# One column of a mean-square kernel loaded ahead of the rest through GpSimd's queue

## The chip, the cores and the metric

The kernel runs on one core of a Trainium2 chip. The core has a matrix engine (unused here), VectorE, ScalarE, GpSimd, SyncE (which only issues transfers here), and 16 DMA engines that move data between the memory (HBM) and the on-chip buffer of 128 partitions. The metric is the device time of one execution in microseconds, as the median of several runs. [...]

## The reference

The input x is 32 x 512 x 1024 values in fp32. For each of the 16,384 rows of 1024 values the variance is wanted:

```
mean_sq = np.mean(x**2, axis=-1)
sq_mean = np.mean(x, axis=-1)**2
return (mean_sq - sq_mean).astype(np.float32)
```

So 67.1 MB are read and 64 KB are written.

## The kernel before, in words

The 16,384 rows are laid out as 128 columns of 128 rows: each partition holds one row (4 KB) of each column. Two blocks give the layout. In the first, 16 columns wide, partition p holds 16 rows of x that follow one another; in the second, 112 columns wide, 112 of them. So `load` (line 40), which loads n neighbouring columns, reads one run of n x 4 KB per partition, 128 runs in all. Every load is issued by SyncE (SP in the profile), in program order, and runs on its queue.

The columns come in two parts. The body is 13 groups of 8 columns (columns 0 to 103), one 4 MB load each, into a pool of three buffers (`xt`). So the load of group g waits until the engines are done with group g - 3. The end is columns 104 to 127, in a buffer of their own (`xt_end`), which no earlier reader holds: loads of 6, 6, 4, 3, 2 and 1 columns (`END_LOADS`, line 62), then columns 126 and 127 as two half loads each.

A column is worked on by VectorE or by ScalarE. VectorE makes statistics of each half of a row (`bn_stats`, line 111), two instructions of 512 elements per column. ScalarE makes two passes over a column (lines 121 and 129): first the negative mean, then the squared deviation, summed into the result tile `mv`. In the body ScalarE takes 3 columns of one group and 2 of the next; in the end the string `END_WHO` says who takes which column (A is ScalarE, D is VectorE); the first of them, column 104, is ScalarE's.

The halves' statistics of the body, and of the first two end loads, are joined into variances by GpSimd in three chains of ten small instructions (`join`, lines 90 to 102): one for the even groups, one for the odd groups, one for the end. For the other end columns VectorE joins them itself (`bn_aggr`, lines 169 and 179).

Two stores write the result: the first block's 16 columns through ScalarE's queue (line 181), the second block's 112 columns through SP's (line 182). In ScalarE's stream the first store stands behind its last body column and ahead of its first end column; it waits for GpSimd's second join, and so does all that follows it on ScalarE. GpSimd issues no transfer; its own stream is four memsets at the start, then the three joins. A scheduler orders each engine's instructions and sets the waits, and it gives the transfers of the SP and ScalarE queues eight completion semaphores in turn, so that a later transfer may wait for the one that used its semaphore before.

Of the kernel before, what the change touches and what calls it, by code (L numbers as in the profile page):

```python
# [11 lines left out]
def kernel(  # L12
# [8 lines left out]
    nc = tc.nc  # L21
    P = nc.NUM_PARTITIONS
# [4 lines left out]
    xf = x.flatten_outer_dims()  # L27
    N, D = xf.shape
# [6 lines left out]
    BLOCKS = [(0, SMALL, 0), (SMALL, ncols - SMALL, SMALL * P)]  # L35

    def block_of(c):
        return next(b for b in BLOCKS if b[0] <= c < b[0] + b[1])

    def load(dst, c0, n, f0=0, f=D):  # L40

        b0, pitch, row0 = block_of(c0)
        assert c0 + n <= b0 + pitch
        ap = [[pitch * D, P], [D, n], [1, f]] if n > 1 else [[pitch * D, P], [1, f]]
        nc.sync.dma_start(  # L45
            out=dst,
            in_=dataclasses.replace(xf, offset=(row0 + c0 - b0) * D + f0, ap=ap),
        )

    def store(engine, block):  # L50
        b0, pitch, row0 = block
        engine.dma_start(
            out=dataclasses.replace(out, offset=row0, ap=[[pitch, P], [1, pitch]]),
            in_=mv[:, 1, b0 : b0 + pitch],
        )
# [3 lines left out]
    END0 = GROUP * NGROUPS  # L59
# [2 lines left out]
    END_LOADS = [6, 6, 4, 3, 2, 1]  # L62
    END_WHO = "AADDDDAADDDDDADDDADADA"
    BATCH = (2, 6, 2)

    xpool = ctx.enter_context(tc.tile_pool(name="xpool", bufs=3))
    spool = ctx.enter_context(tc.tile_pool(name="spool", bufs=4))
# [3 lines left out]
    neg_mean = opool.tile([P, ncols], FP32)  # L71
    junk = [opool.tile([P, D], mybir.dt.bfloat16, name=f"junk{i}") for i in range(4)]
    xt_end = opool.tile([P, ncols - END0, D], FP32)
    stats_of = {}

    def stats_block(name, groups, each):

# [3 lines left out]
    def join(st, groups, each, first, step, skip):  # L81

        n = groups * each
        part = st.rearrange("p n h (e s) -> p n (h e) s", s=3)
        mean, m2 = part[:, :, :, 1], part[:, :, :, 2]
        two = opool.tile([P, n, 2], FP32, name=f"two{first}")
        mu = opool.tile([P, n, 1], FP32, name=f"mu{first}")
        dev = opool.tile([P, n, 4], FP32, name=f"dev{first}")
        g = nc.gpsimd
        g.tensor_tensor(out=two, in0=mean[:, :, 0:2], in1=mean[:, :, 2:4], op=ALU.add)  # L90
        g.tensor_tensor(out=mu, in0=two[:, :, 0:1], in1=two[:, :, 1:2], op=ALU.add)
        g.tensor_scalar(out=mu, in0=mu, scalar1=0.25, scalar2=None, op0=ALU.mult)  # L92
        g.tensor_tensor(out=dev, in0=mean, in1=mu.to_broadcast([P, n, 4]), op=ALU.subtract)  # L93
        g.tensor_tensor(out=dev, in0=dev, in1=dev, op=ALU.mult)  # L94
        g.tensor_scalar(out=dev, in0=dev, scalar1=D / 4.0, scalar2=None, op0=ALU.mult)  # L95
        g.tensor_tensor(out=dev, in0=dev, in1=m2, op=ALU.add)  # L96
        g.tensor_tensor(out=two, in0=dev[:, :, 0:2], in1=dev[:, :, 2:4], op=ALU.add)  # L97
        g.tensor_tensor(out=mu, in0=two[:, :, 0:1], in1=two[:, :, 1:2], op=ALU.add)
        var = mv[:, 1, first : first + groups * step].rearrange(
            "p (g k) -> p g k", k=step  # L100
        )[:, :, skip : skip + each]
        g.tensor_scalar(  # L102
            out=var,
            in0=mu.rearrange("p (g k) o -> p g (k o)", k=each),
            scalar1=1.0 / D,
            scalar2=None,
            op0=ALU.mult,
        )
# [4 lines left out]
    def dve_halves(stats, xcol):  # L113
        dve_half(stats, 0, xcol[:, :H])
        dve_half(stats, 1, xcol[:, H:])

    def act_cols(cols):

        s = D ** -0.5
        for i, (xcol, c) in enumerate(cols):  # L120
            nc.scalar.activation(  # L121
                out=junk[i],
                in_=xcol,
                func=ACTF.Copy,
                scale=-s / D,
                accum_out=neg_mean[:, c : c + 1],
            )
        for i, (xcol, c) in enumerate(cols):
            nc.scalar.activation(  # L129
                out=junk[3],  # L130
                in_=xcol,
                func=ACTF.Square,
                scale=s,
                bias=neg_mean[:, c : c + 1],
                accum_out=mv[:, 1, c : c + 1],
            )
# [6 lines left out]
    for g in range(NGROUPS):  # L143
        c0 = g * GROUP
        xt = xpool.tile([P, GROUP, D], FP32, name="xt")
        load(xt, c0, GROUP)
        skip = ACT_OF_GROUP[g % 2]
        act_cols([(xt[:, k, :], c0 + k) for k in range(skip)])
        st, _, each = body[g % 2]
        for k in range(skip, GROUP):  # L150
            dve_halves(st[:, g // 2 * each + k - skip, :, :], xt[:, k, :])
    for par, (st, groups, each) in enumerate(body):
        join(st, groups, each, par * GROUP, 2 * GROUP, ACT_OF_GROUP[par])

    nb, step, skip = BATCH
    each = step - skip
    st_end = stats_block("stats_end", nb, each)
    k = 0
    for b, n in enumerate(END_LOADS):
        load(xt_end[:, k : k + n, :] if n > 1 else xt_end[:, k, :], END0 + k, n)  # L160
        mine = range(k, k + n)
        act_cols([(xt_end[:, j, :], END0 + j) for j in mine if END_WHO[j] == "A"])
        for j in mine:
            if END_WHO[j] == "D" and b < nb:
                dve_halves(st_end[:, b * each + j - k - skip, :, :], xt_end[:, j, :])
            elif END_WHO[j] == "D":
                stats = spool.tile([P, 2, 6], FP32, name="stats")
                dve_halves(stats, xt_end[:, j, :])
                nc.vector.bn_aggr(out=mv[:, :, END0 + j], in_=stats)  # L169
        if b == nb - 1:  # L170
            join(st_end, nb, each, END0, step, skip)
        k += n
    for j in range(k, ncols - END0):
        stats = spool.tile([P, 2, 6], FP32, name="stats")
        for h in range(2):
            xh = xt_end[:, j, h * H : (h + 1) * H]
            load(xh, END0 + j, 1, h * H, H)
            dve_half(stats, h, xh)
        nc.vector.bn_aggr(out=mv[:, :, END0 + j], in_=stats)  # L179

    store(nc.scalar, BLOCKS[0])
    store(nc.sync, BLOCKS[1])


# [28 lines left out]
```

## Time and profile before

| | us |
|---|---|
| median of 3 runs | 165.49 (165.44 to 165.92) |
| span of the profiled execution | 163.5 |
| VectorE busy | 106.1 (65%) |
| ScalarE busy | 94.9 (58%) |
| GpSimd busy | 10.2 (6%) |
| first body load landed | 12.7 |
| first half of column 126 landed | 157.81 |
| last VectorE instruction ends | 160.84 |
| second store issued | 160.98 |
| second store landed | 162.54 |

The span runs from the first to the last instruction of one execution that the profiler recorded; the runs' median is 2.0 us above it. The busy shares are averages over the whole span. The DMA part of the profile gives the traffic in slices of time, by queue: queue 1 is SP's, queue 10 ScalarE's, queue 14 brings instructions. The packet records give the duration of each row moved, and each of the 16 engines reports the end of its share of a transfer in an event of its own; a transfer has landed with the last of the sixteen. The chain of waits is followed back from the last instruction, at each step to what released it.

### The profile page before, as it was taken

To read this page: it belongs to the slowest core of one execution; us is meant where nothing else is said; L and a number is where in the kernel's file an instruction comes from. 1 tells how busy PE (TensorE), PEld (TensorE's weight loads), DVE (VectorE), ACT (ScalarE), POOL (GpSimd) and SP (SyncE) were. 2 spreads that over 40 slices of the span, in tenths; PEclk is the share of its full clock that TensorE was granted. 3 is DMA by queue.
4 is the path that set the end of the run, shared out by engine and by line. 5 is a ranking of instruction groups with operands and counts; after the bars stand their busy time and mean duration, and the time that the engine had idled before them with its cause. 6 is when DMAs were issued, how large, how long until landed. Compare 5 with 4: busy or idle time off the path is not lost.

```text
span 163.5 us, 462 instructions
## 1 busy us (share of the span) xinstructions
DVE 106.1 (65%) x182; ACT 94.9 (58%) x165; POOL 10.2 (6%) x34
## 2 busy tenths in 40 slices
DVE  0008559393793917949097682949559396859993
ACT  3008756195733937349390693809755195499892
POOL 0000000000000000000000000000000635302200
DMA  7899898998999999999999999999999999999970
GB/s 257 385 481 417 385 513 385 417 481 385 481 417 385 485 409 393 497 393 425 465 393 473 417 393 505 393 401 489 393 465 425 421 391 475 391 440 409 408 291 14
DMA packets 3602, 67.19 MB, mean 411 GB/s; under 512 B 656, under 2 KB 656, under 8 KB 1296
## 3 DMA queue, kind: packets, MB, share of 16 engines
q1 hardware_dynamic: 3456, 67.17, 96.3%
q10 hardware_dynamic: 144, 0.01, 0.1%
q14 instruction: 2, 0.02, 0.0%
HBM read 67.11 MB, written 0.07 MB: 411 GB/s over the span
## 4 chain that ended last, share of the span: by engine, by line
DMA 79%; DVE 11%; ACT 8%; issue 0%; SPq 0%
DMA xt<-in_x_dram 62%; DMA xt_end<-in_x_dram 17%; DVE stats L111 10%; ACT junk L129 4%; ACT junk L121 4%; DVE mv L179 0%; SPq L45 0%
## 5 line engine op out<-in xcount | busy, mean ns | idle before, releaser
L111 DVE BATCH_NORM_STATS2 stats<-xt 128x6 f32<-128x512 f32 x142 | 85.5, 678 | 50.7 <-DMA xt<-in_x_dram 50.7
L121 ACT ACTIVATE junk<-xt 128x1024 bf16<-128x1024 f32 x33 | 34.5, 1046 | 59.2 <-DMA xt<-in_x_dram 59.2
L129 ACT ACTIVATE junk<-xt,neg_mean 128x1024 bf16<-128x1024 f32 x33 | 37.7, 1142 | 0.6
L111 DVE BATCH_NORM_STATS2 stats_end<-xt_end 128x6 f32<-128x512 f32 x16 | 9.7, 680 | 3.7 <-DMA xt_end<-in_x_dram 3.7
L121 ACT ACTIVATE junk<-xt_end 128x1024 bf16<-128x1024 f32 x8 | 8.4, 1046 | 5.0 <-POOL mv L102 4.2
L111 DVE BATCH_NORM_STATS2 stats<-xt_end 128x6 f32<-128x512 f32 x16 | 10.1, 666 | 0.1
L129 ACT ACTIVATE junk<-xt_end,neg_mean 128x1024 bf16<-128x1024 f32 x8 | 9.2, 1144 | 0.2
L90 POOL TENSOR_TENSOR two<-stats 128x72 f32<-128x72 f32 (+1 forms) x2 | 0.8, 406 | 131.3 <-DVE stats L111 131.3
L129 ACT ACTIVATION_READ_ACCUMULATOR junk<-xt,neg_mean 128x1 f32 x33 | 6.2, 186 | 0.0
L121 ACT ACTIVATION_READ_ACCUMULATOR junk<-xt 128x1 f32 x33 | 6.2, 186 | 0.0
L121 ACT ACT_TABLE_LOAD x1 | 1.3, 1283 | 0.7 <-PEq L197 0.7
L121 ACT ACTIVATION_READ_ACCUMULATOR junk<-xt_end 128x1 f32 x8 | 1.5, 186 | 0.0
L129 ACT ACTIVATION_READ_ACCUMULATOR junk<-xt_end,neg_mean 128x1 f32 x8 | 1.5, 186 | 0.0
L95 POOL TENSOR_SCALAR dev<-dev 128x144 f32<-128x144 f32 (+2 forms) x3 | 1.4, 472 | 0.3
L169 DVE BATCH_NORM_AGGREGATE mv<-stats 128x2 f32<-128x12 f32 x6 | 1.2, 203 | 0.1
L94 POOL TENSOR_TENSOR dev<-dev 128x144 f32<-128x144 f32 (+2 forms) x3 | 1.1, 362 | 0.2
L96 POOL TENSOR_TENSOR dev<-dev,stats 128x144 f32<-128x144 f32 (+1 forms) x2 | 1.1, 528 | 0.2
L93 POOL TENSOR_TENSOR dev<-stats,mu 128x144 f32<-128x144 f32 (+1 forms) x2 | 0.9, 470 | 0.2
L102 POOL TENSOR_SCALAR mv<-mu 128x36 f32<-128x36 f32 (+2 forms) x3 | 0.9, 287 | 0.3
L92 POOL TENSOR_SCALAR mu<-mu 128x36 f32<-128x36 f32 (+2 forms) x3 | 0.9, 284 | 0.3
L97 POOL TENSOR_TENSOR two<-dev 128x72 f32<-128x72 f32 (+2 forms) x3 | 0.8, 276 | 0.2
L90 POOL TENSOR_TENSOR two<-stats_end 128x16 f32<-128x16 f32 x1 | 0.2, 233 | 8.9 <-DVE stats_end L111 8.9
(9 smaller groups left out, 2.7 us busy)
## 6 DMA issues: line engine op xcount, KB each, us to landing
xt<-in_x_dram SPq DMA_DIRECT2D x13, 4096.0 KB, 22.2
xt_end<-in_x_dram SPq DMA_DIRECT2D x2, 3072.0 KB, 32.2
xt_end<-in_x_dram SPq DMA_DIRECT2D x1, 2048.0 KB, 40.0
xt_end<-in_x_dram SPq DMA_DIRECT2D x1, 1536.0 KB, 43.2
xt_end<-in_x_dram SPq DMA_DIRECT2D x1, 1024.0 KB, 45.1
xt_end<-in_x_dram SPq DMA_DIRECT2D x4, 256.0 KB, 15.3
xt_end<-in_x_dram SPq DMA_DIRECT2D x1, 512.0 KB, 36.7
out_dram<-mv SPq DMA_DIRECT2D x1, 56.0 KB, 1.6
```

The source lines that it names most:

```text
L90: g.tensor_tensor(out=two, in0=mean[:, :, 0:2], in1=mean[:, :, 2:4], op=ALU.add)
L92: g.tensor_scalar(out=mu, in0=mu, scalar1=0.25, scalar2=None, op0=ALU.mult)
L93: g.tensor_tensor(out=dev, in0=mean, in1=mu.to_broadcast([P, n, 4]), op=ALU.subtract)
L94: g.tensor_tensor(out=dev, in0=dev, in1=dev, op=ALU.mult)
L95: g.tensor_scalar(out=dev, in0=dev, scalar1=D / 4.0, scalar2=None, op0=ALU.mult)
L96: g.tensor_tensor(out=dev, in0=dev, in1=m2, op=ALU.add)
L97: g.tensor_tensor(out=two, in0=dev[:, :, 0:2], in1=dev[:, :, 2:4], op=ALU.add)
L102: g.tensor_scalar(out=var, in0=mu.rearrange("p (g k) o -> p g (k o)", k=each), scalar1=1.0 / D, scalar2=None, op0=ALU.mult,)
L111: nc.vector.bn_stats(out=stats[:, h, :], in_=xh)
L121: nc.scalar.activation(out=junk[i], in_=xcol, func=ACTF.Copy, scale=-s / D, accum_out=neg_mean[:, c : c + 1],)
L129: nc.scalar.activation(out=junk[3], in_=xcol, func=ACTF.Square, scale=s, bias=neg_mean[:, c : c + 1], accum_out=mv[:, 1, c : c + 1],)
L169: nc.vector.bn_aggr(out=mv[:, :, END0 + j], in_=stats)
```

## The change

Column 104 is taken out of the first end load, which then has five columns instead of six. It is loaded by three transfers that GpSimd issues as its first work after the memsets: partitions 0 to 3, partitions 4 to 111, and partitions 112 to 127, each one row of 4 KB per partition. `load` is given a first partition, a number of partitions and an engine for that. Column 104 stays with ScalarE; its first pass now waits for the three transfers, and the scheduler places it ahead of the last two second-pass instructions of ScalarE's body columns. The first store goes from ScalarE's queue to GpSimd's, where it stands behind the second join and ahead of the third. SP's loads keep their order. An unused variable goes.

```
-    def load(dst, c0, n, f0=0, f=D):
+    def load(dst, c0, n, f0=0, f=D, p0=0, p=P, engine=nc.sync):
...
-        ap = [[pitch * D, P], [D, n], [1, f]] if n > 1 else [[pitch * D, P], [1, f]]
-        nc.sync.dma_start(
+        ap = [[pitch * D, p], [D, n], [1, f]] if n > 1 else [[pitch * D, p], [1, f]]
+        engine.dma_start(
             out=dst,
-            in_=dataclasses.replace(xf, offset=(row0 + c0 - b0) * D + f0, ap=ap),
+            in_=dataclasses.replace(
+                xf, offset=(row0 + p0 * pitch + c0 - b0) * D + f0, ap=ap
+            ),
         )
...
+    SHARES = (4, 108, 16)
...
-    stats_of = {}
+
+    p0 = 0
+    for p in SHARES:
+        load(xt_end[p0 : p0 + p, 0, :], END0, 1, p0=p0, p=p, engine=nc.gpsimd)
+        p0 += p
...
-        load(xt_end[:, k : k + n, :] if n > 1 else xt_end[:, k, :], END0 + k, n)
+        own = 0 if k else 1
+        load(
+            xt_end[:, k + own : k + n, :] if n > 1 else xt_end[:, k, :],
+            END0 + k + own,
+            n - own,
+        )
...
-    store(nc.scalar, BLOCKS[0])
+    store(nc.gpsimd, BLOCKS[0])
     store(nc.sync, BLOCKS[1])
```

## The prediction

> **What bounds the kernel now.** I read the chain of waits first. It says that the input stream, and not an engine, sets the end:
>
> ```profile
> DMA 79%; DVE 11%; ACT 8%; issue 0%; SPq 0%
> DMA xt<-in_x_dram 62%; DMA xt_end<-in_x_dram 17%; DVE stats L111 10%; ACT junk L129 4%; ACT junk L121 4%; DVE mv L179 0%; SPq L45 0%
> ...
> 130.17 27.64 DMA xt_end<-in_x_dram
> 157.81 0.02 issue
> 157.83 1.38 DVE stats L111 x2
> 159.21 0.02 issue
> 159.24 0.21 DVE mv L179
> 159.45 1.16 DVE stats L111 x2
> 160.60 0.02 issue
> 160.63 0.21 DVE mv L179
> ```
>
> The last lines are the chain in order of time (start, length, what). The end loads stream until 157.81 us, when the first half of column 126 lands; from there VectorE works without a break to 160.84, and the second store and the close take the rest of 163.5.
>
> Second, the DMA part: 67.11 MB read from HBM, nearly all on queue 1. Its packet records give the prices I use below: a 32 KB row takes 1213 ns, a 24 KB row 916, a 4 KB row 160, a semaphore write 9. The 16 engines stream back to back, sixteen rows at a time, eight rows of every 128-row load on each engine.
>
> Third, the stretches at the two ends (columns: window, length, VectorE, ScalarE, GpSimd busy, clock, DMA share, GB/s):
>
> ```profile
> 1.00:1.50 0.50, 0.00 (x0) 0.50 (x1) 0.00 (x0) 1.00 0.00 0
> 1.50:2.00 0.50, 0.00 (x0) 0.50 (x1) 0.00 (x0) 1.00 3.09 852
> ...
> 158.00:158.25 0.25, 0.25 (x1) 0.25 (x3) 0.00 (x0) 1.00 0.98 361
> 158.25:158.50 0.25, 0.25 (x1) 0.25 (x2) 0.00 (x0) 1.00 0.35 123
> 158.50:158.75 0.25, 0.25 (x2) 0.25 (x1) 0.00 (x0) 1.00 0.13 49
> 158.75:159.00 0.25, 0.25 (x1) 0.25 (x1) 0.00 (x0) 1.00 0.09 33
> 159.00:159.25 0.25, 0.22 (x2) 0.25 (x2) 0.00 (x0) 1.00 0.06 25
> 159.25:159.50 0.25, 0.25 (x2) 0.22 (x2) 0.00 (x0) 1.00 0.00 0
> ```
>
> Nothing moves before 1.7 us (packets are booked where they start, hence 852). At the end one 32 KB row per 1213 ns is 27 GB/s for one engine, so 49, 33 and 25 GB/s are two engines, then one, working alone for some 0.75 us. The completion events of the last half load agree: fourteen engines report from 158.70 to 158.98, one at 159.33, one at 159.76. Going back through the loads, the gap opens between the loads landing at 51.7 and 62.2 us, and in that stretch two 8 KB packets of the instruction queue run, at 55.84 and 57.08:
>
> ```profile
> q1 hardware_dynamic: 78, 2.56, 100.3%
> q14 instruction: 2, 0.02, 0.7%
> ```
>
> So two engines are late, by 0.35 and 0.78 us against the last of the punctual ones, for the rest of the run. Every load counts as landed only when its slowest engine is done; the 157.81 above is the late engine's.
>
> Last, the waits. VectorE's 144.78, 149.70 and 157.83 starts are each released by a landing, with 2.47, 0.07 and 0.25 us idle ahead; ScalarE runs from the landing at 153.35 to 160.59 almost without a gap. If all landings come earlier by d, both engines shift by d, and so does the end.
>
> **The change, part by part.**
>
> *Column 104 through GpSimd.* The bytes stay the same; 512 KB leave the first end load (six columns become five, rows of 24 KB become 20 KB) and go ahead of everything. On each engine that takes 8 x (1213 - 916)/2 = 8 x 149 ns = 1.19 us out of the queue near 130 us. What comes in instead depends on who carries the 4, 108 and 16 rows. If a transfer is dealt out in equal whole rows, as the 128-row loads are, 4 rows are 1 on each of 4 engines, 108 are 9 on each of 12, 16 are 1 on each of 16. If the 4 and the 12 are different engines, four carry 2 rows and twelve carry 10. Ten 4 KB rows and three semaphore writes are 1.60 + 0.03 = 1.63 us: a net +0.44. Two rows are 0.35: a net -0.84. If both late engines are among the four, the slowest goes from 159.76 to 158.92, and the last of the other twelve from 158.98 to 159.42. The gain is d = 159.76 - 159.42 = 0.34 us.
>
> Bounds of d without that assumption: if the two late engines carried none of column 104, the others would have 9.1 rows, net +0.30, d = 0.48; if they carry ten rows like most, d = -0.44; an even split of eight gives -0.12. I take 0.34, because equal whole rows is how every load of this trace is dealt.
>
> [...]
>
> *What it pushes back.* The column goes ahead of the thirteen body loads, so these land about 1.2 us later. VectorE waits 50.7 us in all for them, and the next issue on SP comes 7 us after a landing with two 9.7 us loads still queued, so the stream does not run dry. The last body load lands at about 131.4 instead of 130.15; VectorE's ten halves (6.03 us) and the idle 1.27 after them end at the old 137.47, when the next load lands. Zero, with that 1.27 us as the cover; were it gone, VectorE still has 2.47 us before 144.78.
>
> *The three issues on GpSimd.* GpSimd does nothing from 0.42 to 127.77 us, so even tens of us of descriptor work hold nobody. ScalarE's first pass over column 104 waits for all three transfers, but it stands about 134 us in. Zero.
>
> *The first store.* It leaves ScalarE, which loses a 4.20 us wait for GpSimd's line 102 and 0.37 us of issue. ScalarE gains nothing at the end, since its last stretch starts at a landing. It joins GpSimd behind the second join, at about 142 us; behind it stands only the third join, which waits for VectorE until 149.7, takes 3.1 us, and is needed by the second store at 160.98: some 7 us of cover for the issue, 8 more behind the join. Its landing took 9.0 us before, which would be 151. On SP a 12.1 us wait for this store goes away:
>
> ```profile
> SPq L45 <- DMA out_dram<-mv: 12.1, 1, 12.1
> ```
>
> The two half loads issued after that wait landed 9.4 us after issue with the queue always full, so their earlier issue brings nothing. The store's rows stay 64 B, 11 ns each. Zero.
>
> *What of the cost of GpSimd's queue.* There is no row for it. The lower bound is a gain: if its first rows move in the dead time before 1.72 us, or in the excess of the first rows (1.6 to 2.0 us against 1.21), they cost the stream less. The upper bound: each row takes twice a plain 4 KB row, 10 x 0.16 = 1.6 us. I take the plain 160 ns, the nearest row. [...]
>
> **The sum.** The span goes from 163.5 to about 163.15. The runs' median, 165.49, is 2.0 us above the span, and I leave those 2.0 us as they are: 165.49 - 0.34 = 165.15 us.
>
> **The rivals.**
>
> *A, rows in dead time (faster).* GpSimd's first packets start before 2.2 us. The dead time is 1.0 us from issue (0.72) to first packet plus up to 0.7 us in it. If half of the 1.63 us of rows goes there, the gain is 0.34 + 0.8 = 1.1 us: 164.4. For it: the memsets end at 0.42 and nothing blocks GpSimd. Against: the first load on SP needs 1.0 us from issue to packet, and GpSimd's issue would have to be as quick.
>
> *B, costly rows (slower).* [...] With rows at double price the twelve engines gain 1.6 us and the time is 165.15 + 1.6 = 166.75. It decides from (0.34 + 0.50)/10 = 84 ns more per row, that is 244 ns instead of 160. For it: the stream has no spare time at all, 1213 ns row after row. Against: rows of 2 KB to 24 KB all run at plain price.
>
> *C, the change doesn't level anything.* The late engines are not the favoured four, or the split is another: d from -0.44 to 0.1, 165.4 to 165.9.
>
> **How the numbers follow.** My forecast has 0.36, A 0.13, B 0.30, C 0.21. Within 0.3% (0.50 us, about what a measurement of this kernel can tell from no change) lies the forecast's core, most of C and a little of B; faster by more takes A and the forecast's upper side (d to 0.48 plus a little dead time), slower takes nearly all of B and C's edge. That gives 0.23, 0.44, 0.33. The range runs from A's 164.5 to just beyond B's 166.75; the likeliest case alone is 164.9 to 165.4.
>
> **What would show it.** Right: the completion events of the last loads lie within 0.5 us, GB/s falls to 0 within two quarter-microseconds, the chain's end load stops near 157.5, four engines' trains run ahead after 15 us. C: the tail of one or two engines remains. B: 4 KB rows on GpSimd's queue well above 160 ns, or rows of 32 KB above 1213 before 15 us, and the DMA leg of the chain ending after 158.3. A: packets on that queue before 2.2 us. Wrong altogether would be a wait at the close for GpSimd's queue, or the two instruction packets falling elsewhere in the stream.

## The result

The changed kernel takes 168.16 us (median, 167.77 to 168.72) against 165.49 before: a ratio of 1.0167, with a 95% interval of 1.0148 to 1.0186. It is slower by 2.7 us, where 0.34 us less were forecast, and it lies well above 166.75, where the range that was given ended. The profiled execution took 168.10 us with a span of 166.1; the 2.0 us around the span are as before.

The chain of waits of the changed kernel ends as that of before, only later (start, length, what):

```profile
DMA 83%; ACT 8%; DVE 6%; SPq 0%; issue 0%
...
124.28 36.17 DMA xt_end<-in_x_dram
160.45 0.02 issue
160.47 1.34 DVE stats L118 x2
161.81 0.02 issue
161.84 0.21 DVE mv L191
162.05 1.16 DVE stats L118 x2
163.21 0.02 issue
163.23 0.21 DVE mv L191
```

The transfers still set the end. The first half of column 126 landed at 160.45 instead of 157.81, 2.64 us later, and all that follows is as long as it was. No engine turned into the bound and no wait appeared at the close. So the loss has to be in the stream of transfers. The DMA part of the changed kernel shows the new queue beside the old one:

```profile
q1 hardware_dynamic: 3456, 66.64, 95.2%
q0 software_dynamic: 224, 0.53, 0.9%
```

Queue 0 is GpSimd's. It carries 0.8% of the bytes in 0.9% of the engines' time, so its own rows take nothing out of proportion. What they do to the others shows by stretches. First before, then the changed kernel (window, length, VectorE, ScalarE, GpSimd busy, clock, DMA share, GB/s):

```profile
6.00:21.00 15.00, 6.03 (x10) 6.84 (x12) 0.00 (x0) 1.00 1.04 448
21.00:33.00 12.00, 8.04 (x14) 5.38 (x9) 0.00 (x0) 1.00 1.01 437
```

```profile
6.00:21.00 15.00, 6.03 (x10) 6.15 (x11) 0.00 (x0) 1.00 1.03 380
21.00:33.00 12.00, 6.85 (x12) 5.26 (x10) 0.00 (x0) 1.00 1.01 437
```

From 6 to 21 us, while rows run on queue 0 (the packet records have them from 6.07 to 20.4 us), the 16 engines are as busy as before, 1.03 against 1.04, and move 380 GB/s instead of 448. After 21 us the rate is the same, 437. Busy engines that move less have slower packets: a 32 KB row on SP's queue started from 4 to 24 us takes 1354 ns on average, up to 1769, against 1213 before. Spreading each packet's bytes over its duration, the stream falls 2.14 us behind 433 GB/s between 4 and 30 us, and 0.00 before.

The rest of the 2.7 us is that the engines end further apart. The completion events of the last half load lie from 160.71 to 161.35 for fourteen engines, then 161.92 and 162.36. Their median is 2.14 us later than before (160.94 against 158.80), their last 2.61 us (162.36 against 159.75). The two late engines are still there, and the last of them is now 1.42 us behind the median instead of 0.95. Some 0.2 to 0.3 us of this stand there before the two instruction packets run (at 59.46 and 59.60 us here): at the load that lands just ahead of them the last engine is 0.47 us behind the median, against 0.25 before (0.17 at the loads ahead of that one). The rest of the difference isn't explained by a run.

### The profile page after: what moved, and what is told of

Read it like the earlier page. It is cut to its first block, busy times and chain, and to the rows that moved or that the text cites. A ratio compares the mean times of both kernels' runs of the same rounds, so it can differ in the third digit from the quotient of the medians.

```text
span 166.1 us, 469 instructions
## 1 busy us (share of the span) xinstructions
DVE 106.1 (64%) x182; ACT 95.0 (57%) x165; POOL 12.6 (8%) x38
## 4 chain that ended last, share of the span: by engine, by line
DMA 83%; ACT 8%; DVE 6%; SPq 0%; issue 0%
DMA xt<-in_x_dram 61%; DMA xt_end<-in_x_dram 22%; DVE stats L118 6%; ACT junk L136 4%; ACT junk L128 4%; SPq L45 0%; DVE mv L191 0%
## 5 line engine op out<-in xcount | busy, mean ns | idle before, releaser
L45 POOL DMA_DIRECT2D xt_end<-in_x_dram x3 | 1.8, 601 | 0.8 <-PEq L220 0.8
```

The lines of the kernel that those rows point to most:

```text
L45: engine.dma_start(out=dst, in_=dataclasses.replace(xf, offset=(row0 + p0 * pitch + c0 - b0) * D + f0, ap=ap),)
```

## The experiments

The theory, T, is an assumption: in the three transfers an engine carries other partitions than in the big loads, so it writes to partitions that another engine's big-load rows are going to (such rows are called crossed below), and both are held up. No record names the partition or the engine of a packet, so no run shows which rows are crossed. The rivals: the store on GpSimd's queue (S), any row on GpSimd's queue (Q), the uneven number of rows per engine (U). All edits are against the changed kernel, unless it is said otherwise.

**loads_only.** The store goes back.

```
-    store(nc.gpsimd, BLOCKS[0])
+    store(nc.scalar, BLOCKS[0])
```

> The three GpSimd loads stay, the first store goes back to ScalarE's queue. Theory T (crossed partitions: in the three transfers an engine writes partitions that in the big loads belong to other engines, and while both stream, both slow down): all of the loss is in the loads, 168.0 to 168.3 us, the DMA share of the first 21 us as in the changed kernel (about 363 to 398 GB/s from 8 to 20 us). Rival Q (any row on GpSimd's queue costs the stream): the same. Rival S (the store on GpSimd's queue costs): 165.5 to 167.

Measured: 168.36 us, ratio to before 1.0184 (1.0165 to 1.0203). The whole loss is in the loads.

**store_only.** The kernel before with this one line changed.

```
-    store(nc.scalar, BLOCKS[0])
+    store(nc.gpsimd, BLOCKS[0])
```

> The kernel before with the first store alone moved to GpSimd's queue. Theories T and Q (for the loads): 165.3 to 165.7 us, no change. Rival S (store): above 166.

Measured: 165.54 us, ratio 0.9999 (0.9989 to 1.0008). The store costs nothing and brings nothing; rival S is out.

**one_transfer.** Column 104 stays ahead and on GpSimd's queue, in one piece.

```
-    SHARES = (4, 108, 16)
+    SHARES = (128,)
```

> As the changed kernel, but column 104 in one GpSimd transfer of 128 partitions. Theory T: if 128 rows are dealt as in the big loads, each engine writes its own partitions again; the stream keeps 430 GB/s from 8 us on, time 165.4 to 165.8 (a loss of at most 0.12 for 4 KB rows). Rival Q: the loss stays, 167.5 to 168.3. Rival U (it is the uneven number of rows per engine that costs): 165.4 to 165.8 as well.

Measured: 165.60 us, ratio 1.0004 (0.9994 to 1.0013). The stretch that lost 15% of its rate has all of it again:

```profile
6.00:21.00 15.00, 6.03 (x10) 6.84 (x12) 0.00 (x0) 1.00 1.06 454
21.00:33.00 12.00, 7.22 (x12) 4.56 (x8) 0.00 (x0) 1.00 1.00 431
```

The same 128 rows of 4 KB go through the same queue, from 5.9 to 14.8 us, each at 159 ns. Rival Q is out: neither GpSimd's queue nor loading this column first costs anything that can be measured. The loss is in the cut.

**shares_112_16.** Another cut, even in the number of rows: 112 and 16 are seven times and once the sixteen engines.

```
-    SHARES = (4, 108, 16)
+    SHARES = (112, 16)
```

> [...] Theory T: the loss stays, 167.3 to 168.3. Rival U (uneven rows): 165.4 to 165.9. Rival Q: 167.5 to 168.3.

Measured: 167.35 us, ratio 1.0115 (1.0098 to 1.0131); 384 GB/s from 6 to 21 us. The packet records have its rows in rounds of sixteen, which fits eight on each engine, and still 1.85 us are lost. While only the rows of the 112 partitions run, up to 16.5 us, the stream already falls 1.18 us behind 433 GB/s. Rival U is out as the main cause. It may own the difference to 2.7 us: by 30 us the stream is 1.75 us behind here against 2.14, and the last engine is 1.23 us behind the median against 1.42.

**scalar_queue_shares and scalar_queue_one.** The three transfers, then the one, on ScalarE's queue.

```
-        load(xt_end[p0 : p0 + p, 0, :], END0, 1, p0=p0, p=p, engine=nc.gpsimd)
+        load(xt_end[p0 : p0 + p, 0, :], END0, 1, p0=p0, p=p, engine=nc.scalar)
```

> As the changed kernel, but the three transfers of 4, 108 and 16 partitions are issued on ScalarE's queue instead of GpSimd's. Theory T (crossed partitions): a loss on this queue too, 166.5 to 168.5, with less than 400 GB/s while these rows run. Rival Q (GpSimd's queue itself costs): 165.4 to 165.9.

> As the changed kernel, but column 104 in one 128-partition transfer on ScalarE's queue. Theory T and rival Q: 165.3 to 165.8, since nothing is crossed and GpSimd is not used. If merely a second queue beside SP's, or a column out of order, costs: above 166.5.

Measured: 168.18 us, ratio 1.0163 (1.0148 to 1.0178), and 165.60 us, ratio 1.0006 (0.9996 to 1.0015). The pair repeats on another queue what GpSimd's showed: the cut costs 2.6 us, one piece costs nothing. First the cut, then the one piece, in the same stretch:

```profile
6.00:21.00 15.00, 5.90 (x10) 5.83 (x11) 0.00 (x0) 1.00 1.05 391
```

```profile
6.00:21.00 15.00, 6.03 (x10) 6.84 (x12) 0.00 (x0) 1.00 1.04 446
```

The first of the two also answers what the prediction had assumed. On this queue the 108 rows come twelve at a time in the packet records, and the engines end in three groups: four report the second last half load from 159.94 to 160.33, ten from 161.07 to 161.57, two at 162.16 and 162.21. So here four engines were spared the 108 rows and are ahead by about a microsecond, twelve carried nine of them each, and both late engines are among the twelve. Who carried the four rows of the first transfer, the four engines or some of the twelve, the records don't tell.

**two_columns.** Column 105 as well, in the same shares.

```
-    for p in SHARES:
-        load(xt_end[p0 : p0 + p, 0, :], END0, 1, p0=p0, p=p, engine=nc.gpsimd)
-        p0 += p
+    for j in range(2):
+        p0 = 0
+        for p in SHARES:
+            load(xt_end[p0 : p0 + p, j, :], END0 + j, 1, p0=p0, p=p, engine=nc.gpsimd)
+            p0 += p
...
-        own = 0 if k else 1
+        own = 0 if k else 2
```

> As the changed kernel, but columns 104 and 105 both through GpSimd in shares of 4, 108 and 16. Theory T and rival Q, per row: the loss of 2.7 us doubles, or all but its part that comes from the late engines: 170.0 to 171.0. If the loss is a fixed price of starting GpSimd's queue: 168.1 to 168.5.

Measured: 170.71 us, ratio 1.0332 (1.0301 to 1.0362), 5.2 us above before. Twice the rows in twice the transfers, twice the loss: it grows with what is cut and is no starting price of the queue. Rows and transfers aren't told apart by this run.

**three_by_elements.** Three transfers again, cut along the row, each over all 128 partitions.

```
-    SHARES = (4, 108, 16)
+    SHARES = (128, 768, 128)
...
-    p0 = 0
-    for p in SHARES:
-        load(xt_end[p0 : p0 + p, 0, :], END0, 1, p0=p0, p=p, engine=nc.gpsimd)
-        p0 += p
+    f0 = 0
+    for f in SHARES:
+        load(xt_end[:, 0, f0 : f0 + f], END0, 1, f0, f, engine=nc.gpsimd)
+        f0 += f
```

> As the changed kernel, but the three GpSimd transfers cut column 104 along the row: 128 partitions each, 128, 768 and 128 elements. Theory T: nothing is crossed, 165.4 to 166.0 (24 short rows per engine instead of 8). Rival Q2 (three transfers through GpSimd instead of one cost, whatever they write): 167 to 168.5.

Measured: 165.65 us, ratio 1.0015 (1.0005 to 1.0024). So three transfers instead of one are not the cause; the finer cut costs 0.2 us.

**shares_64_64, shares_32_x4, shares_16_x8.** What sets the price of a cut?

```
-    SHARES = (4, 108, 16)
+    SHARES = (64, 64)
```

with `(32,) * 4` and `(16,) * 8` in the other two.

> As the changed kernel, with two GpSimd transfers of 64 partitions each. [...] If any split of the partitions costs, whoever writes what: 167.1 to 167.7. [...]

Measured: 168.23 us, ratio 1.0141 (1.0112 to 1.0171). This expectation was wrong: the median lies above the range for any split, 167.1 to 167.7, and the loss of 2.6 us is larger than the 1.85 of 112 and 16.

> As the changed kernel, with four GpSimd transfers of 32 partitions each. [...] Theory T2: what counts is how few partitions a transfer's 16 engines write at the same time; 32 partitions at a time cost at least what 64 do, 168.0 to 169.5. [...]

> As the changed kernel, with eight GpSimd transfers of 16 partitions each, one row per engine and transfer. Theory T2: the narrowest, so the dearest, 169 to 172. [...] If the price is per transfer beyond the first: the cut into three along the row cost 0.15 us in all, so eight would add some 0.5, 166.0 to 166.3.

Measured: 167.64 us, ratio 1.0142 (1.0115 to 1.0169), and 169.35 us, ratio 1.0226 (1.0209 to 1.0244). Four times 32 isn't told apart from twice 64 by the intervals; its median is 2.1 us above before, less than T2 had it. Eight times 16 is the dearest by far, 3.85 us, which is against a small price per transfer. So the width of a transfer alone doesn't price all the cuts, and whether the number of crossed rows does can't be said. In this last run the loss can be seen at work:

```profile
GB/s 976 0 218 655 75 908 0 109 765 14 969 0 0 929 55 0 874 0 928 55 0 874 0 819 164 0 874 0 765 218 0 819 55 266 717 0 819 55 819 55
DMA packets 543, 8.91 MB, mean 371 GB/s; under 512 B 160, under 2 KB 160, under 8 KB 287
```

These are its slices from 6 to 30 us; bytes are booked where a packet starts, so the single slices jump, and the mean of 371 GB/s is what counts. By the packet records its sixteen rows per transfer run at 164 ns on average, as good as the plain 160, and after each such round the rate, with the bytes spread over the packets' durations, drops to about 310 to 370 GB/s for some two microseconds and is back at 410 to 430 before the next; only the fourth round comes before the rate has recovered from the third. It is the 32 KB rows that pay, 1454 ns on average for those started from 4 to 24 us.

The costs are within the noise for 128 partitions in one piece (0.04% and 0.06%), 1.15% for 112 and 16, 1.4% for 64 and for 32, and 2.3% for 16. What sets them isn't seen in a trace: whether two engines write the same partitions in the costly runs can't be read from records that name neither the partition nor the engine of a packet. Nor do the runs tell whether the engines get in each other's way at the on-chip buffer or at the memory that they read: a partition and its rows of x go together in all of them. So it is shown that a cut over the partitions costs and that the big rows pay; why they do, T included, stays open.

**shares_on_sp_first.** The three transfers on SP's own queue, ahead of the first body load.

```
-        load(xt_end[p0 : p0 + p, 0, :], END0, 1, p0=p0, p=p, engine=nc.gpsimd)
+        load(xt_end[p0 : p0 + p, 0, :], END0, 1, p0=p0, p=p)
```

> As the changed kernel, but the three transfers of 4, 108 and 16 partitions are issued on SP's queue, ahead of the first body load. Theory T with contention (crossing costs only while the other rows of the same partitions stream): the rows run almost alone, before the big loads, so most of the loss goes: 165.7 to 166.5, what is left from the uneven 2 and 10 rows per engine and the overlap at the edge. If a crossed row is slow in itself, 10 rows at 184 to 344 ns instead of 160: the same range at the low end. If the loss comes from shifting the engines against each other for the whole run: 167 to 168.3.

Measured: 167.13 us, ratio 1.0089 (1.0074 to 1.0105). It misses the expected 165.7 to 166.5. It falls into the range of the third case, engines shifted against each other for the whole run, but the trace doesn't show that case. The loss is smaller than on the other queues and lies at the very start; first before, then this run:

```profile
1.00:3.00 2.00, 0.00 (x0) 1.00 (x1) 0.00 (x0) 1.00 0.92 262
```

```profile
1.00:3.00 2.00, 0.00 (x0) 1.01 (x1) 0.00 (x0) 1.00 0.41 59
```

Three small transfers come through the queue before the first large one, and the engines start late: by the packets' durations some 0.5 us are lost up to 3 us and 0.7 from 3 to 7, and from 7 us on the stream runs at 432. I had left the start out. What in the 0.7 is crossing and what is uneven shares stays open, so this run doesn't decide whether crossed rows cost without a second stream.

## Why the prediction was wrong

**The bound and the path: right.** The stream set the end before and sets it now; VectorE and ScalarE moved along with the landings, by 2.64 us of the 2.67. That also means that what the stream had lost by 30 us was paid in full at 160 us: it was 2.14 us behind there, and the median engine ended 2.14 us later. With the engines streaming back to back (a DMA share of 1.01 from 21 to 33 us and of 1.00 from 33 to 57) there was no gap in which to catch up.

**The step that failed: the price of GpSimd's rows.** "I take the plain 160 ns, the nearest row." The rows themselves were near it, 167 ns in the median. But the step took a row's price as what it takes from its own engine, and the stream paid elsewhere: 2.14 us in slower 32 KB rows. The upper bound of 1.6 us was of the same kind, ten rows at double price, and so too low. Rival B, costly rows, had a chance of 0.30. Two of its signs came true, 32 KB rows above 1213 ns before 15 us (1347 on average from 4 us on) and the chain's transfers ending after 158.3 (160.45). But its price was for the small rows, not for the big ones beside them, and it ended at 166.75. Its argument against, that rows of 2 KB to 24 KB all run at plain price, said nothing: those rows were all of transfers over 128 partitions, and the trace had no other.

**The dealing: wrong for this queue.** Four engines with 2 rows and twelve with 10 were assumed. On GpSimd's queue the 108 rows come in rounds of 16, 16, 16, 15, 15, 15 and 15, which fits seven on each engine but the last, and three there. On ScalarE's queue the 108 rows did go to twelve engines, nine each, as the prediction had assumed for this one.

**The late engines: found, not reached.** Two engines late from the time of two instruction packets on was right, and they are late in all these runs; that the packets make them late was not tested. That they would be among the favoured four was only assumed, and in the run that favours four engines it is not so. So even with plain rows the forecast's levelling would not have come about; the nearest run, column 104 in one piece, ended 0.1 us slower than before, where the prediction's even split of eight rows gave a loss of 0.12. That is rival C.

**What was costed at nothing.** The store: right, 0.9999, although its rows did not stay as they were: on GpSimd's queue they are sixteen of 512 B at 27 to 33 ns, and it landed 5.6 us after its issue. The three issues on GpSimd, 1.8 us in all from 1.25: right, and hidden. The body loads pushed back by about 1.2 us: the first landed at 14.77 instead of 12.72, 2.05 us later, about 1 us of which is the column itself (13.79 with the column in one piece). That cost next to nothing by itself, as forecast: the one piece is 0.1 us slower than before, within the noise. Rival A is out: the first 4 KB row on GpSimd's queue ran at 6.07 us, 4.8 us after its issue, far from the dead time before 2.2.

**Small slips in the working.** VectorE's idle time ahead of 157.83 was 0.04 us, not 0.25, since an aggregate ran until 157.79; all landings moved together, so nothing rested on it. Rival A's sum gives 164.4, and the range calls it 164.5.

No version here beats the kernel before. The harmless form, column 104 in one piece, is the same within 0.1%.

## What to carry to other kernels

In this kernel, where a full stream of 128-partition loads sets the time, a transfer over part of the partitions was not priced by its own bytes or rows: 512 KB cut over the partitions cost 1.85 to 3.85 us on queues beside the stream's and 1.5 us ahead of the stream on its own, and in one piece about 0.1 us, within the noise, on either queue tried. Cut along the row instead, where several transfers are wanted; that cost 0.2 us here. And before work is moved between DMA engines to level them, find out which engines are late and how that queue deals that shape; here neither followed from the trace of another shape (108 rows came sixteen at a time on one queue and twelve at a time on another).

## What the runs showed of the hardware that was not expected

The victim of such a transfer was the other stream: with shares of 16 partitions, sixteen 4 KB rows at 159 to 207 ns each are followed by some two microseconds of 32 KB rows at up to 1768 ns instead of 1213. The two queues deal the same 108 rows differently, sixteen at a time with a remainder on GpSimd's, twelve at a time on ScalarE's. And after two 8 KB instruction packets, near 56 us before and near 59.5 us in the changed kernel, two of the 16 engines are behind the last of the others until the end of the run, by 0.35 and 0.78 us before and by 0.57 and 1.01 us in the changed kernel.
